# Splitting 220 of 493 weight blocks with GpSimd's transfers: a rounding load, then an accumulating one

## The chip, the cores and the metric

The program runs on one core of one Trainium2 chip. The core has TensorE (PE, matrix multiplications), VectorE (DVE), ScalarE (ACT), GpSimd (POOL) and SyncE (SP, which in this program only issues transfers), and 16 DMA engines that all transfers share, whichever engine issues them. Each engine works off its own queue in order and waits for the others by semaphores. The metric is the device time of one execution in microseconds (us); lower is better.

## What is computed

One sequence of 512 tokens and width 1024 goes through two blocks. The first has two layers, each a feed-forward (SwiGLU) half step, a mixer and another feed-forward half step, each behind a modulated RMS norm; the mixer of layer 0 is stick-breaking attention, that of layer 1 a gated linear recurrence. The second block has two hybrid layers, each one large projection, three kinds of attention, gates, and an output projection.

```python
def first_block(...):
    for layer in range(2):
        mod = (silu(c) @ mod_w[layer] + mod_b[layer]).reshape(B, 3, 3, 1024)
        h, g = sublayer_input(x, norm_g[layer, 0], mod[:, 0])
        x = x + 0.5 * g * swiglu(h, ffn_w_gu[layer, 0], ffn_w_down[layer, 0])
        h, g = sublayer_input(x, norm_g[layer, 1], mod[:, 1])
        y = stick_breaking_attention(h, sb_w_qkv, sb_w_o) if layer == 0 else rglru_block(h, lru_w_in, ..., lru_w_out)
        x = x + g * y
        ...                       # and a second swiglu like the first
def hybrid_layer(x, norm_g, w_in, w_br_a, w_br_b, w_br_c, w_out, cos, sin):
    proj = rmsnorm_2(x, norm_g) @ w_in
    ...                           # ya, yb, yc: block-sparse, top-k and dilated attention, each times a silu gate
    merged = gates_a * (ya @ w_br_a) + gates_b * (yb @ w_br_b) + gates_c * (yc @ w_br_c)
    return x + merged @ w_out
```

## The kernel before

The work is transposed: channels stand on the 128 partitions, the 512 tokens along the row. Every matrix product is made nearly exact in three passes. A float32 operand is split into a high part, rounded to the matmul format F32R, and a low part, the rest; `proj` then issues high·high, high·low and low·high into one PSUM bank.

The weights come as a stream. `layout` puts all weights, in the order of use, into blocks of 128 x 1024 float32 (512 KB, eight slots of 128 x 128 each); between them stand 144 blocks of the modulation's matrix, which DVE reduces (L485). The eight stages in order are ffn00, sb (attention), ffn01, ffn10, lru (recurrence), ffn11, hy0, hy1 (hybrid layers).

- `stream_dma` loads the next blocks: SP issues a transfer into a tile `raw`, of which there are four (`RAW = 4`), as soon as one is free (L463).
- `stream_step` splits the next half block (128 x 512): ACT rounds it into `wh` (L497), then POOL or DVE subtracts, `wl` = `raw` - `wh` (L503). Which of the two it is goes by `pool_low`: 1.0 in sb, in most of lru and in the hybrid layers (all to POOL), 0 in the bodies of the feed-forward stages (all to DVE). `wh` and `wl` have five buffers each (`AHEAD + 1`). When both halves are split, the `raw` is free for the next load.
- `take` hands a slot's `wh` and `wl` to a matmul, and before that has the half blocks up to four ahead of it split (`AHEAD = 4`).

So half block c+4 goes into the buffers that half block c-1 leaves, and TensorE starts on it four half blocks after it has left them. The rest of the work (attention units, gates, norms) runs as generators whose instructions are put among the matmuls; a scheduler at build time, which goes by its own estimates of durations, then fixes each engine's order. In sb an attention unit computes two sigmoids on ACT, masks a diagonal block on POOL (`affine_select`, L1132), scans and multiplies on DVE (L1133, L1137) and goes back to TensorE (transposes `T`, products `o`). In the hybrid layers a pair's projection is rotated on DVE (`sw`, `r`, `rL`: L1362 to L1375, with `rH` on ACT), stacked by SP's transfers (`qs`, `ks`, `kl`, L981) and scored into `z` on TensorE, which DVE masks and reduces (L1399). At the end of a hybrid layer come some 29 blocks that are nothing but projections, with sums on POOL (`sig`, L1816).

Of the kernel before, what the change touches and what calls it, by code (L numbers as in the profile page):

```python
# [22 lines left out]
F32 = mybir.dt.float32  # L23
F32R = mybir.dt.float32r
I32 = mybir.dt.int32
AF = mybir.ActivationFunctionType
OP = mybir.AluOpType
# [149 lines left out]
def first_slots(segs):  # L177

    out = {}
    slot = 0  # L180
    for name, jobs, _ in segs:
        for job in jobs:
            for kt in rows_of(job):
                for j, (_, _, cols) in enumerate(job[1]):
                    if name in LATE and job[0] == "first":
                        out[slot] = (LATE[name], kt, j)
                    elif name == "ffn00" and job[0] in ("gu6", "gu7"):
                        out[slot] = ((0, 0), kt, int(job[0][2:]))
                    slot += len(cols) // 128
    return out  # L190


def rows_of(job):
    return range(job[2]) if isinstance(job[2], int) else job[2]
# [120 lines left out]
class Kern:  # L315
# [117 lines left out]
    def stream_init(self, entries):  # L433
        self.entries = entries
        self.e_dma = 0
        self.e_conv = 0
        self.raws = {}
        self.parts = {}
        self.slot = 0
        self.w_conv = 0  # L440
        self.n_w, self.kept = 0, []
        self.in_ring = 0
        self.full = set()
        self.wshift = {}
        self.inv = None
        self.look = self.AHEAD
        self.act_busy = False
        self.pool_low = 0.0
        self.pool_credit = 0.0

    def stream_dma(self):
        nc = self.nc
        while self.e_dma < len(self.entries):
            src = self.io["ws"][self.e_dma]
            e = self.entries[self.e_dma]
            if e[0] == "w" and self.n_w < self.KEEP:
                raw = [self.t("keep"), self.t("keep")]
                self.n_w += 1
                for j in range(2):
                    nc.sync.dma_start(raw[j], src[:, 512 * j:512 * j + 512])  # L460
            elif self.in_ring < self.RAW:
                raw = self.wpool.tile([128, 1024], F32, name=self.name("raw"), tag="raw", bufs=self.RAW)
                nc.sync.dma_start(raw, src)  # L463
                self.in_ring += 1
                if e[:2] == ("mod", (0, 0, 1)):
                    x = self.t("x")
                    nc.sync.dma_start(x, self.io["xT"][e[2]])
                    if e[2] == 4:
                        nc.sync.dma_start(self.ident, self.io["k_ident"])
                    self.x.append(x)  # L470
            else:
                break
            self.raws[self.e_dma] = raw
            self.e_dma += 1

    def stream_step(self):
        self.stream_dma()
        e = self.entries[self.e_conv]
        raw = self.raws[self.e_conv]
        nc = self.nc  # L480
        if e[0] == "mod":
            vec, m = e[1], e[2]
            if vec not in self.mods:
                self.mods[vec] = self.modp.tile([128, 8], F32, name=self.name("mod"), tag="mod", bufs=12)
            nc.vector.tensor_tensor_reduce(raw, raw, self.cact, 1.0, 0.0, OP.mult, OP.add, accum_out=self.mods[vec][:, m:m + 1])  # L485
            self.full.add((vec, m))
            if m == KD - 1 and vec != (0, 0, 1):
                self.mod_end(vec, 0, KD)
        else:
            j = self.w_conv % 2  # L490
            w = raw[j] if type(raw) is list else raw[:, 512 * j:512 * j + 512]
            h = self.wpool.tile([128, 512], F32R, name=self.name("wh"), tag="wh", bufs=self.AHEAD + 1)
            l = self.wpool.tile([128, 512], F32R, name=self.name("wl"), tag="wl", bufs=self.AHEAD + 1)
            if self.act_busy:
                nc.vector.tensor_copy(h, w)
            else:
                nc.scalar.copy(h, w)  # L497
            self.pool_credit += self.pool_low
            eng = nc.vector
            if self.pool_credit >= 1.0:  # L500
                self.pool_credit -= 1.0
                eng = nc.gpsimd
            eng.tensor_tensor(l, w, h.bitcast(F32), OP.subtract)  # L503
            self.parts[self.w_conv] = (h, l)
            if type(raw) is list:
                self.kept.append((4 * self.w_conv, w))
            else:
                self.shifts(w, 4 * self.w_conv)
            self.w_conv += 1
            if j == 0:  # L510
                return
        if type(raw) is not list:
            self.in_ring -= 1
        del self.raws[self.e_conv]
        self.e_conv += 1
        self.stream_dma()
# [41 lines left out]
    def take(self, n):  # L558
        c, o = divmod(self.slot, 4)
        self.ahead(c)  # L560
        self.parts.pop(c - 1, None)
        self.slot += n
        h, l = self.parts[c]
        return h[:, 128 * o:128 * (o + n)], l[:, 128 * o:128 * (o + n)]
# [1334 lines left out]
    def body(self):  # L1899
        nc = self.nc  # L1900
        segs = segments()
        self.stream_init(layout(segs))
        self.segs = {n: list(j) for n, j, _ in segs}
        self.late = first_slots(segs)
        self.mods = {}
        self.twice = False
        self.quick = False
        self.sq = {}
        self.gain, self.save, self.hnext, self.xd = None, False, [], []
        self.vecs = self.const.tile([128, NVEC], F32, name="vecs")  # L1910
        self.ident = self.const.tile([128, 128], F32, name="ident")
        self.ones = self.const.tile([128, 128], F32, name="ones")
        self.cact = self.const.tile([128, 1024], F32, name="cact")

        def shown(name):
            if self.upto == name:
                for m in range(KD):
                    nc.sync.dma_start(self.io["out"][m], self.x[m])
                return True

        for l in range(2):
            for i in range(2):
                self.jobs = self.segs[f"ffn{l}{i}"]
                if (l, i) == (1, 1):
                    self.twice = self.save = True
                    self.fgain = self.modp.tile([128, 8], F32, name="gain")
                    nc.vector.tensor_tensor(self.fgain, self.vec("final_norm_g"), self.vec("norm_g_2", 0, 8), OP.mult)
                self.ffn(l, i)
                if shown(f"ffn{l}{i}"):
                    return  # L1930
                if i:
                    continue
                if l == 0:
                    self.jobs = self.segs["sb"]
                    self.stick()
                else:
                    with self.tc.manual_schedule():
                        self.lru_consts()
                    self.jobs = self.segs["lru"]
                    self.lru()  # L1940
                if shown("sb" if l == 0 else "lru"):
                    return
        self.hybrid_consts()
        for l in range(2):
            self.jobs = self.segs[f"hy{l}"]
            self.hybrid(l)
            if shown(f"hy{l}"):
                return
        self.last_norm()
# [28 lines left out]
```

## Time and profile before

| | us |
|---|---|
| median of 3 runs | 3132.27 (3131.87 to 3133.31) |
| the profiled execution | 3133.14 |
| its span, first to last instruction | 3131.3 |
| TensorE busy in it | 3007.2 |
| VectorE busy | 1921.7 |
| ScalarE busy | 1321.7 |
| GpSimd busy | 1072.8 |

A profile gives for each engine when each instruction ran; an instruction's idle time before it is put down to what released it. Matmuls overlap each other, so their mean duration (0.39 us) is longer than their distance.

### The profile page before, as it was taken

What the parts mean: (1) busy time and instruction counts of PE and PEld (TensorE: products, weight loads), DVE (VectorE), ACT (ScalarE), POOL (GpSimd) and SP (SyncE); (2) the same over time, 40 slices, a digit from 0 to 9 for tenths busy, and PEclk for the clock granted to TensorE, in tenths of its full rate; (3) what the DMA queues carried; (4) which work ended last, traced back from release to release, by engine and by line L of the source; (5) the groups of instructions that cost most, each with busy time, mean ns of one, the idle gap of its engine ahead of it and who ended that gap; (6) DMA issues with size and microseconds to landing.
All of it is one profiled execution on the core that took longest, in us unless ns stands there. A gap on an engine that the chain in (4) does not pass through costs nothing. (4 is left out here: it accounts for less than half of the span.)

```text
span 3131.3 us, 39192 instructions
## 1 busy us (share of the span) xinstructions
PE 3007.2 (96%) x13752; PEld 2474.4 (79%) x13752; DVE 1921.7 (61%) x3455; ACT 1321.7 (42%) x2520; POOL 1072.8 (34%) x828
## 2 busy tenths in 40 slices
PE   7999999989999999999899999999999999999998
PEld 5788877778888888887788888888787778878776
DVE  7844467685445654569773334587766547877643
ACT  3332245543332333226543333355455434655552
POOL 4455744440001100025430002433334674333356
PEclk9999999999999999999999999999999999999999
DMA  6454545324343344542222223543441336324322
GB/s 243 163 195 172 209 120 142 102 68 147 130 140 128 135 162 149 181 175 74 88 88 101 94 105 111 136 135 105 120 132 62 108 124 177 103 88 128 102 78 91
DMA packets 132358, 400.03 MB, mean 128 GB/s; under 512 B 18496, under 2 KB 19008, under 8 KB 132160
## 3 DMA queue, kind: packets, MB, share of 16 engines
q1 hardware_dynamic: 132160, 397.51, 39.1%
q8 instruction: 109, 1.79, 0.2%
q14 instruction: 89, 0.73, 0.1%
HBM read 342.91 MB, written 6.30 MB: 112 GB/s over the span
## 5 line engine op out<-in xcount | busy, mean ns | idle before, releaser
L503 POOL TENSOR_TENSOR wl<-raw,wh 128x512 fp32r<-128x512 f32 x576 | 803.0, 1402 | 940.9 <-ACT wh L497 897.2
L497 ACT CAST wh<-raw 128x512 fp32r<-128x512 f32 x968 | 596.4, 620 | 1152.7 <-PE mm L417 993.0
L417 PE MATMUL mm<-hH,wh 128*128 128x512 f32 x1584 | 620.9, 392 | 12.4 <-ACT ge L1284 9.8
L417 PE MATMUL mm<-hL,wh 128*128 128x512 f32 x1584 | 620.3, 392 | 4.1 <-DVE hL L722 3.4
L417 PE MATMUL mm<-hH,wl 128*128 128x512 f32 x1584 | 619.4, 391 | 0.3 <-POOL wl L503 0.3
L503 DVE TENSOR_TENSOR wl<-raw,wh 128x512 fp32r<-128x512 f32 x394 | 290.0, 737 | 363.0 <-ACT wh L497 360.6
L417 PE MATMUL mm<-gH,wh 128*128 128x512 f32 x1016 | 409.7, 403 | 1.9 <-ACT wh L497 1.8
L417 PE MATMUL mm<-gH,wl 128*128 128x512 f32 x1016 | 401.9, 396 | 1.3 <-POOL wl L503 1.3
L417 PE MATMUL mm<-gL,wh 128*128 128x512 f32 x1016 | 401.6, 395 | 0.0
L417 PEld LDWEIGHTS mm<-hH,wh 128*128 128x128 f32 x1584 | 299.1, 189 | 76.0 <-ACT ge L1284 10.2
L417 PEld LDWEIGHTS mm<-hL,wh 128*128 128x128 f32 x1584 | 299.0, 189 | 68.5 <-DVE hL L722 5.5
L417 PEld LDWEIGHTS mm<-hH,wl 128*128 128x128 f32 x1584 | 298.9, 189 | 62.3 <-POOL wl L503 0.7
L485 DVE CUSTOM_DVE_ANT_0 raw<-raw,cact 128x1024 f32<-128x1024 f32 x144 | 209.2, 1456 | 177.4 <-DMA raw<-ws 167.0
L417 PE MATMUL mm<-aH,wh 128*128 128x512 f32 x704 | 273.9, 389 | 0.0
L417 PE MATMUL mm<-aH,wl 128*128 128x512 f32 x704 | 273.9, 389 | 0.0
L635 POOL TENSOR_TENSOR sq<-x 128x512 f32<-128x512 f32 x7 | 8.1, 1151 | 736.9 <-DVE x L970 710.0
L417 PEld LDWEIGHTS mm<-gH,wl 128*128 128x128 f32 x1016 | 192.4, 189 | 42.1 <-POOL wl L503 2.6
L417 PEld LDWEIGHTS mm<-gH,wh 128*128 128x128 f32 x1016 | 193.4, 190 | 36.2 <-ACT wh L497 2.3
L417 PEld LDWEIGHTS mm<-gL,wh 128*128 128x128 f32 x1016 | 193.3, 190 | 32.9
L1029 DVE TENSOR_TENSOR wide<-T,wide 128x128 fp32r<-128x128 f32 (+3 forms) x192 | 94.2, 511 | 102.5 <-ACT wide L1026 93.8
L417 PEld LDWEIGHTS mm<-aH,wh 128*128 128x128 f32 x704 | 132.1, 188 | 27.6
L417 PEld LDWEIGHTS mm<-aH,wl 128*128 128x128 f32 x704 | 132.1, 188 | 27.4
(302 smaller groups left out, 4825.0 us busy)
## 6 DMA issues: line engine op xcount, KB each, us to landing
raw<-ws SPq DMA_DIRECT2D x629, 512.0 KB, 3.3
ks<-rH SPq DMA_DIRECT2D x80, 128.0 KB, 3.1
kl<-rL SPq DMA_DIRECT2D x80, 128.0 KB, 2.4
qs<-rH SPq DMA_DIRECT2D x56, 128.0 KB, 3.9
qs<-rL SPq DMA_DIRECT2D x56, 128.0 KB, 3.9
keep<-ws SPq DMA_DIRECT2D x16, 256.0 KB, 5.7
ks<-qkH SPq DMA_DIRECT2D x32, 128.0 KB, 2.8
kl<-qkL SPq DMA_DIRECT2D x32, 128.0 KB, 2.4
```

The lines of the kernel that those rows point to most:

```text
L417: self.nc.tensor.matmul(out, lhsT, rhs, start=start, stop=stop, skip_group_check=True)
L485: nc.vector.tensor_tensor_reduce(raw, raw, self.cact, 1.0, 0.0, OP.mult, OP.add, accum_out=self.mods[vec][:, m:m + 1])
L497: nc.scalar.copy(h, w)
L503: eng.tensor_tensor(l, w, h.bitcast(F32), OP.subtract)
L635: nc.gpsimd.tensor_tensor(q, self.x[m], self.x[m], OP.mult)
L1029: nc.vector.tensor_tensor(dst(pt[1], o, n, step), src(c, n, step), dst(pt[0], o, n, step).bitcast(F32), OP.subtract)
```

## The change

In the four stages sb, lru, hy0 and hy1, 220 blocks are handled in another way: all but those in which a slot also goes into the shift vectors of a norm (`late`). Their load is issued by POOL, with F32R as its destination, so that the transfer itself rounds: the tile `raw` is then the high part, and no `wh` is written. For each half, ACT writes minus the high part into `wl` (`scalar.mul` by -1.0), and a second transfer, issued by POOL too, reads the same half block from HBM again and adds it into `wl`. The `raw` tile now holds what the matmuls read, so it goes back to the ring not when it is split but when `take` has gone past its second half (`held`).

Counted over the program, 422 subtractions on POOL and 18 on DVE go, and 440 roundings on ACT become 440 multiplications (2 of the roundings stood on DVE). SP issues 220 loads less. POOL issues 660 transfers, 220 of 512 KB and 440 of 256 KB, where it issued none. 110 MiB more are read from HBM.

```diff
+def inlined(segs, entries, names, late):
+    out = set()
+    ...
+    for i, e in enumerate(entries):
+        if e[0] != "w":
+            continue
+        name = next((name for end, name in ends if slot < end), None)
+        if name in names and not any(slot + j in late for j in range(8)):
+            out.add(i)
+        slot += 8
+    return out
...
+            elif e[0] == "w" and self.in_ring < self.RAW and self.inline(self.e_dma):
+                raw = self.wpool.tile([128, 1024], F32, name=self.name("raw"), tag="raw", bufs=self.RAW)
+                nc.gpsimd.dma_start(raw.bitcast(F32R), src)
+                raw = (raw, src)
+                self.in_ring += 1
...
+    INLINE = "sb", "lru", "hy0", "hy1"
+    def inline(self, e):
+        return e in self.inlined
...
+            if type(raw) is tuple:
+                h = raw[0].bitcast(F32R)[:, 512 * j:512 * j + 512]
+                l = self.wpool.tile([128, 512], F32R, name=self.name("wl"), tag="wl", bufs=self.AHEAD + 1)
+                nc.scalar.mul(l, h.bitcast(F32), -1.0)
+                nc.gpsimd.dma_start(l, raw[1][:, 512 * j:512 * j + 512], accum_op=OP.add)
+                self.parts[self.w_conv] = (h, l)
+                self.w_conv += 1
+                if j == 0:
+                    return
+                self.held.append(self.w_conv)
+                del self.raws[self.e_conv]
+                self.e_conv += 1
+                self.stream_dma()
+                return
...
         self.parts.pop(c - 1, None)
+        while self.held and self.held[0] <= c:
+            self.held.pop(0)
+            self.in_ring -= 1
+        self.stream_dma()
```

POOL's queue near the end of hy0's attention, where the projections begin (`sig` are the sums of the gated branches). Before:

```order
L1816 TENSOR_TENSOR sig_17890<-sig_17890,sig_19706 128x512
L503 TENSOR_TENSOR wl_20310<-raw_20030,wh_20309 128x512
L1816 TENSOR_TENSOR sig_17995<-sig_17995,sig_19790 128x512
L503 TENSOR_TENSOR wl_20340<-raw_20030,wh_20339 128x512
L1816 TENSOR_TENSOR sig_18245<-sig_18245,sig_19876 128x512
L1816 TENSOR_TENSOR sig_18348<-sig_18348,sig_19954 128x512
L503 TENSOR_TENSOR wl_20375<-raw_20093,wh_20374 128x512
```

The same place of the changed kernel (its lines have other numbers: L483 is the rounding load, L527 the accumulating one, L1866 the sum):

```order
L1866 TENSOR_TENSOR sig_17713<-sig_17713,sig_19479 128x512
L483 DMA raw_20068<-ws 128x1024
L527 DMA wl_20065<-ws 128x512
L1866 TENSOR_TENSOR sig_17813<-sig_17813,sig_19561 128x512
L1866 TENSOR_TENSOR sig_18058<-sig_18058,sig_19645 128x512
L527 DMA wl_20096<-ws 128x512
L1866 TENSOR_TENSOR sig_18156<-sig_18156,sig_19721 128x512
L483 DMA raw_20131<-ws 128x1024
L1866 TENSOR_TENSOR sig_18383<-sig_18383,sig_19788 128x512
L527 DMA wl_20128<-ws 128x512
```

Where two subtractions stood for a block, three issues stand, a load first; the load waits for TensorE to leave the block four before it, the accumulating one for ACT's multiplication, and the sums wait behind them.

POOL's queue in sb, between the masks of the attention units. Before:

```order
L503 TENSOR_TENSOR wl_5386<-raw_5073,wh_5385 128x512
L1132 AFFINE_SELECT beta_5353<-beta_5353 128x128
L1132 AFFINE_SELECT beta_5402<-beta_5402 128x128 x2
L503 TENSOR_TENSOR wl_5428<-raw_5073,wh_5427 128x512
L503 TENSOR_TENSOR wl_5481<-raw_5140,wh_5480 128x512
```

And in the changed kernel (L1182 is the mask):

```order
L527 DMA wl_5465<-ws 128x512
L1182 AFFINE_SELECT beta_5482<-beta_5482 128x128
L483 DMA raw_5497<-ws 128x1024
L527 DMA wl_5494<-ws 128x512
L1182 AFFINE_SELECT beta_5482<-beta_5482 128x128
L1182 AFFINE_SELECT beta_5529<-beta_5529 128x128
```

A mask can now stand behind a load that waits for TensorE.

## Rows read from the trace of the kernel before

**Rows 1.** The page, part 1: each engine's busy time, share of the span, instructions.
```profile
PE 3007.2 (96%) x13752; PEld 2474.4 (79%) x13752; DVE 1921.7 (61%) x3455; ACT 1321.7 (42%) x2520; POOL 1072.8 (34%) x828
```

**Rows 2.** Windows (sb, lru, ffn11, hy0, hy1): PE, PEld, DVE, ACT, POOL busy, clock, DMA share, GB/s.
```profile
403.00:671.00 268.00, 250.61 (x1210) 204.77 (x1209) 190.07 (x309) 144.07 (x286) 119.48 (x128) 0.97 0.40 111
...
1405.00:1610.00 205.00, 187.78 (x807) 152.66 (x806) 162.41 (x193) 111.54 (x176) 98.25 (x68) 0.96 0.24 84
1610.00:1973.00 363.00, 362.73 (x1612) 300.43 (x1611) 155.98 (x225) 124.33 (x204) 39.88 (x29) 1.00 0.29 102
1973.00:2537.00 564.00, 540.44 (x2601) 444.34 (x2600) 383.05 (x884) 284.42 (x620) 254.85 (x195) 0.99 0.39 114
2537.00:3114.00 577.00, 560.04 (x2683) 461.01 (x2681) 369.17 (x857) 283.11 (x618) 272.18 (x213) 0.99 0.36 110
```

**Rows 3.** TensorE's waits in lru: us in total, times, longest.
```profile
PE mm L417 <- ACT ge L1284: 9.8, 1, 9.8
PE z L417 <- DVE xL L1252: 4.2, 1, 4.2
...
PE T L417 <- POOL wl L503: 0.7, 1, 0.7
```

**Rows 4.** TensorE's waits in hy0.
```profile
PE z L417 <- DVE mx L1399: 5.0, 5, 2.3
PE T L421 <- ACT T L1417: 3.5, 8, 0.9
PE o L417 <- DVE diag L663: 2.7, 1, 2.7
...
PE z L417 <- DMA ks<-rH: 0.5, 1, 0.5
```

**Rows 5.** POOL's groups in hy0: count, busy us, mean ns, idle before.
```profile
L503 POOL TENSOR_TENSOR wl<-raw,wh 128x512 fp32r<-128x512 f32 x159 | 214.8, 1355 | 306.2 <-ACT wh L497 294.7 <-PE mm L417 3.5 <-PE o L417 3.2
```

**Rows 6.** DVE's groups in hy0, two that read two SBUF tiles, one PSUM.
```profile
L1366 DVE TENSOR_TENSOR sw<-sw,rope 128x512 f32<-128x512 f32 x24 | 27.5, 1146 | 0.0
L1375 DVE TENSOR_TENSOR rL<-r,rH 128x512 fp32r<-128x512 f32 x24 | 26.6, 1110 | 10.8 <-ACT rH L1373 10.6
...
L1029 DVE TENSOR_TENSOR wide<-T,wide 128x512 fp32r<-128x512 f32 x24 | 16.5, 686 | 27.6 <-ACT wide L1026 27.6
```

**Rows 7.** DVE in ffn10, two SBUF tiles read, while POOL has little to do.
```profile
L928 DVE TENSOR_TENSOR aL<-a,aH 128x512 fp32r<-128x512 f32 x10 | 6.9, 692 | 0.8
```

**Rows 8.** Timeline in hy0: start us, us, engine, line, instruction.
```profile
2042.89 2.98 POOL L503 TENSOR_TENSOR wl<-raw,wh 128x512 fp32r<-128x512 f32 x2 [2.73 <-ACT wh L497]
...
2043.19 1.53 DVE L1366 TENSOR_TENSOR sw<-sw,rope 128x512 f32<-128x512 f32 x1
...
2044.65 1.77 DVE L1375 TENSOR_TENSOR rL<-r,rH 128x512 fp32r<-128x512 f32 x1
```

**Rows 9.** Timeline of ACT in hy0's projections.
```profile
2477.07 0.62 ACT L497 CAST wh<-raw 128x512 fp32r<-128x512 f32 x1 [2.11 <-PE mm L417]
...
2479.78 0.62 ACT L497 CAST wh<-raw 128x512 fp32r<-128x512 f32 x1 [1.11 <-PE mm L417]
2482.51 0.62 ACT L497 CAST wh<-raw 128x512 fp32r<-128x512 f32 x1 [2.11 <-PE mm L417]
```

**Rows 10.** Timeline of POOL at the same place.
```profile
2480.48 1.29 POOL L503 TENSOR_TENSOR wl<-raw,wh 128x512 fp32r<-128x512 f32 x1 [1.42 <-ACT wh L497]
```

**Rows 11.** DMA issues of the whole span: count, KB each, median us to landing.
```profile
raw<-ws SPq DMA_DIRECT2D x629, 512.0 KB, 3.3
...
kl<-rL SPq DMA_DIRECT2D x80, 128.0 KB, 2.4
```

**Rows 12.** The tile raw, late in hy0: duration ns of SP's issue, min/median/max.
```profile
L463 SPq DMA_DIRECT2D raw<-ws x18: 327/328/390, 2410.1 to 2526.0; - x18
```

**Rows 13.** Window with the densest small transfers, the start of hy0.
```profile
1973.00:2100.00 127.00, 121.70 (x628) 103.77 (x627) 88.29 (x215) 58.90 (x124) 53.03 (x42) 1.00 0.58 148
```

**Rows 14.** ACT's groups in lru: loads of a function table, count, busy us, mean ns.
```profile
L1277 ACT ACT_TABLE_LOAD x4 | 5.1, 1283 | 0.1
```

More of the change, by code (lines that the diff above doesn't have):

```diff
@@ L189, in first_slots @@
                     slot += len(cols) // 128
+    return out
+def inlined(segs, entries, names, late):
+    out = set()
+    ends = []
+    n = 0
+    for name, jobs, _ in segs:
+        n += sum(len(cols) // 128 for job in jobs for _ in rows_of(job) for _, _, cols in job[1])
+        ends.append((n, name))
+    slot = 0
+    for i, e in enumerate(entries):
[5 more added lines that the diff above has]
+        slot += 8
     return out
@@ L446, in stream_init @@
         self.look = self.AHEAD
+        self.held = []
         self.act_busy = False
@@ L1904, in body @@
         self.late = first_slots(segs)
+        self.inlined = inlined(segs, self.entries, self.INLINE, self.late)
         self.mods = {}
```

## The prediction

> **What bounds the kernel now.** I read the page first: TensorE is busy 96% of the span [rows 1], so only what shortens TensorE's waits can gain, and whatever adds waits costs. Then the windows by stage: the feed-forward stages leave it next to nothing (362.73 of 363 us in ffn11), and the change leaves them alone. In the four stages that it touches, the waits are 268 - 250.6 = 17.4 us in sb, 17.2 in lru, 23.6 in hy0 and 17.0 in hy1, 75.2 together [rows 2]. That is all there is to gain. Third, the waits: hardly any is for a weight. In lru the long ones are for the recurrence's own chain, and one of 0.7 us for `wl`; in hy0 they are for DVE's masks and reductions, ACT's softmax, a norm's factors [rows 3, 4]. Weights are ready early: in pure projections ACT rounds a half block every 2.72 us, as soon as TensorE has left the buffer, and POOL's subtraction ends 2.0 us later (2479.78 to 2480.48 + 1.29), while TensorE wants it after four half blocks, 4 x 2.72 = 10.9 us [rows 9, 10]. So the split as such is hidden, and the change must gain or lose through its side effects.
>
> **Part by part: what goes.** POOL's subtractions took 1.36 us each in hy0, 215 us of its 255 [rows 2, 5]. POOL waits for TensorE's releases most of the time, so its own time is worth nothing. But DVE pays: with two SBUF tiles to read, its 512-wide operation takes 0.69 us where POOL is nearly idle [rows 7], 1.15 and 1.11 us in hy0, where an operation that reads PSUM still takes 0.69 [rows 6]. The timeline shows how: two subtractions run on POOL from 2042.89 to 2045.87, and `sw` and `rL` on DVE take 1.53 and 1.77 us beside them [rows 8]. These two groups alone lose 24 x (1.15 + 1.11 - 2 x 0.69) = 21 us in hy0.
>
> How much of that reaches TensorE? The operations that TensorE waits for are mostly not stretched themselves, they stand behind one that is. A wait for the masked scores is 5.0 / 5 = 1.0 us [rows 4], a stretch 1.11 - 0.69 = 0.42 us on the mean [rows 6, 7]; if six in ten waits stand behind a stretched operation, a quarter goes. A quarter of 75.2 is **-19 us**; bounds 0 (DVE's time is off the path) and -40 (half the waits go).
>
> **What is replaced at no price.** ACT's rounding, 0.62 us [rows 9], becomes a multiplication of the same 512 columns; nothing. SP's issues fall away; SP bounds nothing, TensorE's waits for its stacks are 0.5 us in hy0 [rows 4]. Two more loads of a function table stand in ACT's order in lru, 1.28 us each [rows 14], **+3 us** at most; I take all of it.
>
> **What is added: the chain behind a half block.** No transfer issued by POOL and none that accumulates is in this trace, so both get bounds. Issue: between 0.33 us, what SP takes [rows 12], and 1.29 us, what POOL took for its subtraction [rows 10]; I take 0.8, and two of them one behind the other, since the load can stand before the accumulating one. Landing: 2.4 us for 128 KB, 3.3 for 512 KB issued by SP [rows 11]. An accumulating 256 KB reads source and destination, so I price it as 512 KB: 3.3 us. Sum: 0.62 + 1.6 + 3.3 = 5.5 us against 10.9, hidden. Upper bound: both issues at 1.29 and the landing behind that of a load, 0.62 + 2.6 + 6.6 = 9.8, still hidden, with 1.1 us to spare: there the cover is thin. The load itself is issued when TensorE leaves a block and wanted three blocks, 6 x 2.72 = 16.3 us, later, after 0.8 + 3.3 for itself and 5.5 for what follows. **0 us**, and the risk goes into a rival.
>
> **The transfer engines.** In ffn11, nearly all loads of blocks, 102 GB/s take a share of 0.29, so a full engine set moves 352 GB/s; in the densest mix of small transfers 148 at 0.58, 255 GB/s [rows 2, 13]. A block of 0.52 MB takes 1.5 us of the set now. Its two accumulations take between 1.5 us (like a plain load) and 4.1 us (twice the bytes at 255 GB/s); taken 3.0, twice at 352. So 4.5 us (3.0 to 6.2) stand against 5.44 us a block in pure projections, and 564 / 82 = 6.9 on hy0's mean, where 0.39 x 6.9 - 1.5 = 1.2 us a block of other transfers come on top. Taken: 83% full in both, enough. At the upper bound it isn't.
>
> The Trainium skill, "Collectives: The Full Stack", section "The bandwidth ceiling: the fold count and why AG ≠ RS ≠ AR", says that an add in the transfer engines costs no cycles of its own but two source reads on one ring, so half the rate. By that an accumulation counts twice, which is what I took from the rows; had it counted once, the block would cost 3.0 us. No row before shows one.
>
> **Sum.** -19 + 3 = -16 on the profiled execution's 3133.1: 3117; the median of the runs shown is 0.9 lower, so **3116 us**, with its own range of 3100 to 3126.
>
> **The rivals.**
> 1. *The low part comes late* (slower). Place: the pure projections of hy0, hy1 and lru, and wherever stacks fill the transfer queues. It decides from 10.9 us from TensorE's release to landing, or 5.44 us of transfer engines a block. For it: my upper bounds are 9.8 and 6.2 us, and all prices are borrowed from SP's transfers; every issue also waits in one in-order queue with POOL's sums and masks. Against it: the middle values are 5.5 and 4.5. Price: at 6.2 us a block, 0.75 us on some 110 blocks of pure projections is +83, so 3132 - 16 + 83 = 3199; with rounding at half rate too it is 3.0 + 4.1 = 7.1 us, 8.3 with the 1.2 of other transfers, and 164 hybrid blocks at 1.4 us over the mean give +230.
> 2. *The gain doesn't arrive.* DVE's freed 21 us a hybrid layer lie in queue time that TensorE never sees, or issuing on POOL stretches DVE as subtracting did. For it: the longest wait of all, 9.8 us, ends with ACT [rows 3]. 3132 to 3135.
> 3. *POOL's queue gets in the way.* A load waits at its head for TensorE, and sb's masks and the hybrid sums stand behind it. For it: before, the subtractions waited too, but with 306 us of idle time in hy0 [rows 5] no one was behind them for long. If a third of the 75 us of waits grow by as much again, +25 - 16: 3141.
> 4. *More gain.* Half the waits go, -40 + 3: 3095.
>
> The Trainium skill, "SBUF — State Buffer", section "SBUF: two separate sides", has a rule against the change: while DVE runs an operation in its two-port mode, such as an fp32 copy in SBUF, GpSimd can't write the descriptors of its transfers, and they start late. Here that would add to rival 1's chain, one DVE operation of up to 0.69 us for each of two issues [rows 7]: 9.8 + 1.4 = 11.2 us at the upper bound, past 10.9; 6.9 at the middle, hidden. No row here shows it, since nothing was issued there.
>
> **How the numbers follow.** Forecast 0.37, rival 4 0.10, rival 2 0.15, rival 1 0.30, rival 3 0.08. Faster or slower by 0.2% is 6 us, about what a measurement of this kernel can tell. Faster: 0.37 + 0.10 = 0.47; same: 0.15; slower: 0.30 + 0.08 = 0.38. The range runs from 3085, under rival 4, to 3205, just over rival 1's first price; it leaves out its heavier form and what is better than rival 4.
>
> **What would show it.** Right: no `wl` subtraction on POOL in the four stages but those near their starts; `sw` and `rL` near 0.69 us; an accumulating transfer landing within 4 us of its issue; TensorE's waits in hy0 and hy1 at 30 us together instead of 41, none worth naming on `wl` or `raw`. Wrong: waits of TensorE on transfers into `wl`, ACT's multiplication waiting for `raw`, a share of the transfer engines near 0.9 in the projections (rival 1); unstretched DVE and unchanged waits (2); masks or sums on POOL idle behind an issue (3).

## The result, and the profile after

The changed kernel takes **3165.24 us** (median of 4 runs, 3153.11 to 3167.03) against 3132.79 for the kernel before beside it: ratio 1.0091, 95% interval 1.0075 to 1.0106. Slower by 32 us, where 16 us faster was forecast. The profiled execution took 3167.03, its span is 3165.2.

Part 1 of its page (as [rows 1]):

```profile
PE 3018.0 (95%) x13752; PEld 2479.5 (78%) x13752; DVE 1804.7 (57%) x3435; ACT 1324.1 (42%) x2524; POOL 994.7 (31%) x1066
```

The windows of sb, lru, ffn11, hy0 and hy1, columns as in [rows 2]:

```profile
406.00:681.00 275.00, 255.37 (x1212) 208.03 (x1211) 175.96 (x311) 145.04 (x286) 105.87 (x157) 0.95 0.72 161
1413.00:1616.00 203.00, 187.54 (x804) 151.51 (x803) 124.13 (x174) 115.50 (x179) 95.39 (x109) 0.97 0.74 153
1616.00:1982.00 366.00, 364.48 (x1613) 301.81 (x1612) 155.94 (x224) 124.47 (x204) 45.07 (x35) 1.00 0.32 103
1982.00:2558.00 576.00, 543.31 (x2601) 445.46 (x2600) 354.71 (x884) 283.58 (x619) 220.58 (x273) 0.99 0.84 183
2558.00:3148.00 590.00, 561.26 (x2682) 462.71 (x2681) 338.12 (x857) 283.05 (x619) 239.93 (x295) 0.99 0.86 184
```

Two things happened at once. VectorE is relieved (hy0: 383 to 355 us busy, hy1: 369 to 338). But TensorE waits more: length less busy time is 19.6 + 15.5 + 32.7 + 28.7 = 96.5 us in the four stages, against 75.2 in [rows 2], and the transfer engines stand at 0.72 to 0.86. The stages grow by 7 us (sb), 12 and 13 us (the hybrids); lru is 2 shorter.

Half of TensorE's waits now end with a transfer: 48.8 of the 96.5 us in the four stages, against 1.6 us before. Two thirds of them are for weights (`wl` and `raw`, 33.5 us) and a third for stacks (15.3 us, 9.9 of them in sb). The waits on transfers (us, times, longest):

```profile
PE mm L436 <- DMA wl<-ws: 27.6, 19, 4.7
PE z L436 <- DMA kl<-qkL: 6.3, 3, 2.9
PE mm L436 <- DMA raw<-ws: 3.6, 1, 3.6
PE z L436 <- DMA ks<-qkH: 3.6, 2, 3.1
PE z L436 <- DMA kl<-rL: 3.0, 2, 1.5
PE z L436 <- DMA qs<-rL: 2.4, 1, 2.4
PE T L436 <- DMA wl<-ws: 1.2, 1, 1.2
PE o L436 <- DMA wl<-ws: 1.1, 1, 1.1
```

The DMA issues of the page (count, KB each, median us to landing) show how long a transfer now takes: `kl` lands in 7.0 us for 2.4 in [rows 11], `ks` in 6.3 for 3.1, `qs` in 5.1 for 3.9.

```profile
raw<-ws POOLq DMA_DIRECT2D x220, 512.0 KB, 5.3
wl<-ws POOLq DMA_DIRECT2D x440, 256.0 KB, 5.4
ks<-rH SPq DMA_DIRECT2D x80, 128.0 KB, 6.3
kl<-rL SPq DMA_DIRECT2D x80, 128.0 KB, 7.0
qs<-rH SPq DMA_DIRECT2D x56, 128.0 KB, 5.1
```

The two DVE groups of [rows 6] in hy0 are short again, so the stretching was GpSimd's subtractions:

```profile
L1425 DVE TENSOR_TENSOR rL<-r,rH 128x512 fp32r<-128x512 f32 x24 | 19.5, 813 | 32.7 <-ACT rH L1423 32.7
L1416 DVE TENSOR_TENSOR sw<-sw,rope 128x512 f32<-128x512 f32 x24 | 16.3, 680 | 0.0
```

And longer waits stand on ScalarE (12.6 us for `raw` before), whose multiplication needs the rounding load:

```profile
ACT wl L526 <- DMA raw<-ws: 142.0, 48, 8.9
ACT wh L543 <- DMA raw<-ws: 35.4, 12, 7.1
```

### The profile page after: what moved, and what is told of

It is laid out like the page before. It is cut to its first block, busy times and chain, and to the rows that moved or that the text cites. A ratio compares the mean times of both kernels' runs of the same rounds, so it can differ in the third digit from the quotient of the medians.

```text
span 3165.2 us, 39232 instructions
## 1 busy us (share of the span) xinstructions
PE 3018.0 (95%) x13752; PEld 2479.5 (78%) x13752; DVE 1804.7 (57%) x3435; ACT 1324.1 (42%) x2524; POOL 994.7 (31%) x1066
## 3 DMA queue, kind: packets, MB, share of 16 engines
q0 software_dynamic: 95040, 230.73, 35.3%
## 5 line engine op out<-in xcount | busy, mean ns | idle before, releaser
L543 ACT CAST wh<-raw 128x512 fp32r<-128x512 f32 x530 | 326.1, 620 | 785.7 <-PE mm L436 679.9
L527 POOL DMA_DIRECT2D wl<-ws x440 | 385.7, 911 | 591.7 <-ACT wl L526 566.1
L436 PE MATMUL mm<-hH,wh 128*128 128x512 f32 x1248 | 486.0, 390 | 0.0
L526 ACT ACTIVATE wl<-raw 128x512 fp32r<-128x512 f32 x440 | 273.1, 629 | 444.8 <-PE mm L436 243.2
L436 PE MATMUL mm<-gH,raw 128*128 128x512 f32 x892 | 362.3, 406 | 1.3 <-DVE sig L1860 1.3
L436 PE MATMUL mm<-gL,raw 128*128 128x512 f32 x892 | 354.2, 397 | 0.0
L549 POOL TENSOR_TENSOR wl<-raw,wh 128x512 fp32r<-128x512 f32 x154 | 227.8, 1494 | 198.2 <-ACT wh L543 183.2
L436 PEld LDWEIGHTS mm<-hL,wh 128*128 128x128 f32 x1248 | 234.7, 188 | 53.2 <-DVE hL L772 4.6
L483 POOL DMA_DIRECT2D raw<-ws x220 | 136.0, 618 | 315.1 <-PE mm L436 252.8
L436 PEld LDWEIGHTS mm<-gH,raw 128*128 128x128 f32 x892 | 170.7, 191 | 31.4 <-DVE sig L1860 2.2
L436 PEld LDWEIGHTS mm<-gL,raw 128*128 128x128 f32 x892 | 170.6, 191 | 28.2
```

The lines of the kernel that those rows point to most:

```text
L436: self.nc.tensor.matmul(out, lhsT, rhs, start=start, stop=stop, skip_group_check=True)
L483: nc.gpsimd.dma_start(raw.bitcast(F32R), src)
L526: nc.scalar.mul(l, h.bitcast(F32), -1.0)
L527: nc.gpsimd.dma_start(l, raw[1][:, 512 * j:512 * j + 512], accum_op=OP.add)
```

## The experiments

**Two runs that take the two halves apart.** `e1_no_sub`: the kernel before without the subtractions. (In the code of all runs, `...` stands for lines left out.)

```diff
-            eng.tensor_tensor(l, w, h.bitcast(F32), OP.subtract)
+            if self.e_conv in self.inlined:
+                l = h
+            else:
...
+                eng.tensor_tensor(l, w, h.bitcast(F32), OP.subtract)
```

> The kernel before, with the subtractions of the 220 blocks left out: the matmuls read the high part a second time where they read the low part, so the low part of these weights is missing from the result. No transfer is added. It sizes the relief of DVE alone. Theory (relief is worth what TensorE's other waits lost in the changed kernel, 75 to about 48 us): 3132 - 27 = 3105 us, 3098 to 3115, with TensorE's waits in sb, lru, hy0 and hy1 at 45 to 55 us and `sw` and `rL` near 0.69 us. Rival (DVE's time is off the path, and the waits of the changed kernel only moved to the transfers): 3126 to 3134 us, though `sw` and `rL` are short.

Measured: 3065.55 us, ratio to before 0.9776 (0.9763 to 0.9790). The relief is 70 us, over twice what the theory gave. Over the four stages TensorE's waits for VectorE fall from 44 us to 12 and those for ScalarE from 26 to 13; for GpSimd it had hardly waited (1.6 us). So most of the relief comes by way of VectorE.

`e2_no_acc`: the changed kernel without its accumulating transfers.

```diff
-                nc.gpsimd.dma_start(l, raw[1][:, 512 * j:512 * j + 512], accum_op=OP.add)
```

> The changed kernel without the accumulating transfers: `wl` stays minus the high part, so the low part of these weights is wrong. Rounding loads, their place in GpSimd's queue, the ring of four held tiles and ScalarE's multiplication all stay. Theory (the accumulating transfers fill the transfer engines and make stacks and low parts late): the stacks `ks`, `kl`, `qs` land within 4 us of their issue again, the share of the transfer engines in hy0 and hy1 falls from 0.85 to 0.5 or less, and the time is that of the relief, 3103 to 3115 us. Rival (the loads in GpSimd's in-order queue, held back by the ring, cost it): TensorE's waits on ScalarE's multiplication and on masks stay, 3125 to 3150 us.

Measured: 3068.92 us, ratio 0.9791 (0.9777 to 0.9804). So rounding loads, the ring of held tiles and their place in GpSimd's queue cost next to nothing, the relief is 66 us, and **the accumulating transfers, with all that waits for them, cost 3165 - 3069 = 96 us**. Its windows (sb, lru, hy0, hy1):

```profile
409.00:660.00 251.00, 244.56 (x1209) 200.77 (x1208) 170.50 (x309) 144.51 (x286) 55.40 (x99) 0.99 0.44 116
1393.00:1582.00 189.00, 182.93 (x806) 149.75 (x805) 124.56 (x175) 112.19 (x177) 48.36 (x53) 0.99 0.28 87
1945.00:2486.00 541.00, 533.18 (x2601) 443.80 (x2600) 344.56 (x884) 285.69 (x620) 85.75 (x114) 1.00 0.43 118
2486.00:3050.00 564.00, 553.93 (x2683) 460.18 (x2681) 332.31 (x856) 284.33 (x618) 93.94 (x126) 1.00 0.43 115
```

TensorE's waits here are 6.4 + 6.1 + 7.8 + 10.1 = 30.4 us, 45 less than before, and its busy time is 1514.6 us for 1538.9, another 24 less, for the same matmuls. About half of the second part is the clock: by its records, the granted clock stood at 0.50 for 47.8 us of these stages before (TensorE busy in 40.7) and for 17.0 us here (15.5). At half the clock a busy microsecond does about half the work (12 matmuls for 23 in 5 us, below), so (40.7 - 15.5) / 2 = 12.6 us go with it; what the other half is was not found. In lru of the changed kernel TensorE waits 4.75 us for a `wl`, until 1525.20. Windows before the wait, right behind it, and later show what follows:

```profile
1515.00:1520.40 5.40, 3.78 (x16) 2.53 (x14) 5.02 (x8) 5.36 (x10) 0.58 (x2) 1.00 0.61 146
1525.20:1530.20 5.00, 5.00 (x12) 3.94 (x13) 4.23 (x7) 2.58 (x5) 1.27 (x2) 0.50 1.06 186
1531.00:1536.00 5.00, 5.00 (x23) 4.10 (x22) 2.35 (x4) 3.36 (x6) 1.84 (x3) 1.00 0.61 148
```

Behind the wait the granted clock is 0.50 (1.2 of 2.4 GHz) and 12 matmuls start in 5 us, later 23. That wait cost 4.75 us and some 2.5 more.

Stage by stage the changed kernel is 99 us longer than `e2_no_acc` in the four windows: 32 us are waits on `wl` and `raw`, 13 waits on stacks, 21 other waits, and 33 more busy time for the same matmuls, 22 of them by the clock, worked out as above.

**Runs that were to split the 96 us, and showed ScalarE's queue.** `e3_acc_scratch`:

```diff
-    NSLOT = 74
+    NSLOT = 72
...
             eng.tensor_tensor(l, w, h.bitcast(F32), OP.subtract)
+            if self.e_conv in self.inlined:
+                src = self.io["ws"][self.e_conv][:, 512 * j:512 * j + 512]
+                nc.gpsimd.dma_start(self.scratch[self.w_conv % 2], src, accum_op=OP.add)
```

> The kernel before, complete, plus the 440 accumulating transfers of 256 KB, each issued behind its subtraction into one of two scratch tiles that nothing reads (72 tiles in the arena for 74 to make room). Nobody waits for these transfers. Theory (the transfer engines' queueing is the loss, and the stacks its first victim): the stacks land at 5 to 7 us for 2.4 to 3.1, TensorE waits 10 to 25 us longer on `ks`, `kl` and `qs`, 3143 to 3160 us. Rival (only the low parts' own chain is late; the stacks are hidden): 3132 to 3138 us, what the issues on GpSimd cost.

Measured: 3644.57 us, ratio 1.1625 (1.1609 to 1.1640), outside both. The transfers depended on no weight, only on the scratch tile, so they were not paced with TensorE; GpSimd's waits and TensorE's:

```profile
POOL scratch L525 <- DMA scratch<-ws: 613.2, 374, 5.5
```

```profile
PE mm L436 <- POOL wl L522: 360.8, 18, 311.3
```

The subtractions of hy0 stood in GpSimd's queue behind transfers that waited for each other, and TensorE stood once for 311.3 us. The run says nothing of contention, but how dear a waiting issue in an in-order queue can be.

`e4_look66` (`NSLOT`: tiles of 128 x 512 in the arena that the rest of the work draws on):

```diff
-    NSLOT = 74
+    NSLOT = 70
...
-    RAW = 4
+    RAW = 6
...
+    LOOK = 6
...
+                tag = ("wh", "wl")[j]
...
+        while (self.w_conv < c + 1 + self.LOOK and self.e_conv in self.raws and type(self.raws[self.e_conv]) is tuple
+               and self.look == self.AHEAD and all(i in self.single for i in range(c, self.w_conv))):
             self.stream_step()
```

> The changed kernel with more time for the same transfers: six `raw` tiles for four, and the low parts of inlined blocks started up to six half blocks ahead for four, in the buffers of `wh` and `wl` in turn (70 tiles in the arena for 74). Same transfers, same bytes. Theory A (the chain of the low part is too long for its cover; its queueing varies): TensorE's waits on `wl` and `raw`, 33 us of the 49 on transfers, nearly go, those on stacks stay: 3132 to 3145 us. Theory B (the transfer engines are full, more time doesn't help, or the earlier start makes the stacks later still): 3158 to 3175 us. Theory C (all of the loss was the short cover): 3105 to 3120 us.

Measured: 3394.49 us, ratio 1.0816 (1.0793 to 1.0839), worse than any theory. `e5_unread`:

```diff
-                self.parts[self.w_conv] = (h, l)
+                self.parts[self.w_conv] = (h, h)
```

> The changed kernel with all its transfers, but the matmuls read the high part a second time where they read the low part of the 220 blocks; the low parts are written and never read (they are missing from the result). So no wait of TensorE on `wl` is left, and the load on the transfer engines stays. Without any accumulating transfer the time is 3069 us, with them 3165 us: 96 us to be split. Theory (late low parts are the smaller part; the stacks, the raw blocks that ScalarE waits for, and the clock that falls with the waits are the larger): 3115 to 3145 us, with waits on `ks`, `kl` and `qs` in sb and the hybrids still near 16 us. Rival (the low part's own lateness is nearly all of it): 3069 to 3085 us.

Measured: 3551.20 us, ratio 1.1323 (1.1304 to 1.1341), outside both. `e6_whole`:

```diff
+                h = raw[0].bitcast(F32R)
+                l = self.wpool.tile([128, 1024], F32R, name=self.name("wl"), tag="w", bufs=self.AHEAD + 1)
                 nc.scalar.mul(l, h.bitcast(F32), -1.0)
...
+                nc.gpsimd.dma_start(l, raw[1], accum_op=OP.add)
...
```

> The changed kernel with one accumulating transfer of 512 KB a block in place of two of 256 KB (rows of 4 KB for 2 KB), one multiplication of 1024 columns in place of two of 512, in tiles that take the place of `wh` and `wl` with the same bytes. Theory A (an accumulating row has a fixed price, so a 4 KB row costs less than two of 2 KB at 178 ns): the share of the transfer engines in the hybrids falls to 0.65 to 0.75, and the time to 3100 to 3140 us. Theory B (the price goes by bytes): rows of 350 ns, the share stays at 0.84, 3150 to 3180 us, the longer transfers weighing against the fewer issues.

Measured: 3443.09 us, ratio 1.0985 (1.0963 to 1.1006), outside both. In these three the same row of ScalarE's waits grew; here that of `e4_look66`, of `e5_unread` and of `e6_whole`:

```profile
ACT wl L529 <- DMA raw<-ws: 396.1, 105, 16.7
```

```profile
ACT wl L526 <- DMA raw<-ws: 853.1, 184, 12.5
```

```profile
ACT wl L526 <- DMA raw<-ws: 711.0, 171, 11.8
```

From 52.1 us in `e2_no_acc` (3069) over 142 in the changed kernel (3165) to 396 (3394), 711 (3443) and 853 (3551), a longer wait goes with a longer time, though not in proportion. In the changed kernel the multiplication waits for a buffer that TensorE must leave, which keeps it late. With more buffers, or with buffers that nobody reads, that hold is gone: in `e5_unread` it waits for TensorE 7.2 us in 5 places, in the changed kernel 243.2 us in 174. It then stands earlier in ScalarE's order, which the build fixes by its own estimates. ScalarE comes to it a median of 6.0 us after its load's issue in the changed kernel, but of 2.5, 2.2 and 1.9 us in `e4_look66`, `e6_whole` and `e5_unread`, and the load takes 5.3 to 6.2 us to land. Casts and softmax queue behind it: in `e5_unread` TensorE waits 83.7 us, 34 times, for softmax values `T` from ScalarE. So none of the three tells late low parts from load. `e6_whole` does tell the price: its queue of GpSimd's transfers took 30.3% of 16 engines' 3443.5 us; with the rounding rows as in `e2_no_acc` (13.0% of 3066.8 us for 28,160 of them, 0.23 us each), an accumulating 4 KB row takes (16694 - 6380) / 28160 = 0.37 us, and one of 2 KB in the changed kernel (35.3% of 3165.2 us) (17877 - 6380) / 56320 = 0.20 us. The price goes by bytes, as theory B had it.

`e7_alternate`:

```diff
-        return e in self.inlined
+        return e in self.inlined and e % 2 == 0
```

> The changed kernel with only every second of the 220 blocks split by transfers, the others by ScalarE and GpSimd as before. Theory (the relief goes by the number of subtractions that leave GpSimd, half of 66 us; the loss by queueing, which falls faster than the load): 3100 to 3125 us, share of the transfer engines in the hybrids about 0.62, stacks landing at 3 to 5 us. Rival (both halve): (3133 + 3165) / 2 = 3149 us. Rival (GpSimd's in-order queue suffers from the mixture: subtractions behind loads that wait for TensorE): over 3150 us.

Measured: 3156.54 us, ratio 1.0070 (1.0055 to 1.0085), over the theory, 8 us over the rival in which both halve, and in the range of the last one, whose reason (GpSimd's queue) the run with six tiles below speaks against. The stacks are better (`kl` 5.2 us, `ks` 4.0), but now the blocks that ScalarE rounds wait for their loads, since a held tile keeps the ring of four full:

```profile
ACT wh L543 <- DMA raw<-ws: 234.7, 69, 11.7
```

`e8_dve_half`:

```diff
-                eng = nc.gpsimd
+                eng = nc.vector if self.w_conv // 2 % 2 else nc.gpsimd
```

> The kernel before without any new transfer: where GpSimd subtracted, every second block's two subtractions go to VectorE instead. Theory (GpSimd's subtractions cost VectorE more in stretched operations than VectorE would need to do them itself): each one moved adds 0.69 us to VectorE and takes away a stretch of up to 1.1 us that hits some of its operations; 3105 to 3132 us. Rival (VectorE's own queue is what TensorE waits behind, and 75 us more work in each hybrid layer lengthens it): 3135 to 3170 us.

Measured: 3130.39 us, ratio 0.9991 (0.9982 to 1.0000). It lies at the upper edge of the theory's range: VectorE pays about what it gets.

**More lead for the loads.** `e9_raw5`, whose edit is shown, `e10_raw6` (6 and 70 in place of 5 and 72) and the same six with every second block, `e11_alt_raw6`:

```diff
-    NSLOT = 74
+    NSLOT = 72
...
-    RAW = 4
+    RAW = 5
```

> The changed kernel with five `raw` tiles for four (72 tiles in the arena for 74): each load is issued one block, about 5.4 us, earlier against ScalarE's multiplication, and nothing else changes; the same transfers and bytes. Theory (ScalarE's in-order queue is where the time goes: its multiplication waits for the rounding load, and softmax, casts and gates wait behind it): ScalarE's waits on `raw` fall from 177 us to under 60, TensorE's waits on transfers and on ScalarE fall with them, 3105 to 3140 us. Rival (the transfer engines are too full, whatever the order: loads issued earlier queue longer and make stacks later): 3155 to 3185 us.

> As the run with five tiles, with six (70 tiles in the arena): loads two blocks, about 10.9 us, earlier than in the changed kernel. Theory (ScalarE's queue): ScalarE's waits on `raw` nearly gone, 3095 to 3130 us; what is left above 3069 us is the stacks' and the low parts' own lateness. Rival (full transfer engines): 3155 to 3190 us. A third way (70 tiles are too few, TensorE waits for attention units that wait for tiles): over 3150 us with short waits of ScalarE on `raw`.

> Every second block split by transfers, as in the alternating run (3157 us, where ScalarE waited 235 us for `raw`, since a held tile keeps the next load back), with six `raw` tiles and 70 in the arena. Theory (ScalarE's queue): its waits on `raw` fall below 40 us and the time to 3085 to 3115 us, under both kernels: half the relief of 66 us, and stacks that land at 3 to 5 us. Rival (queueing or the mixture on GpSimd decides): 3135 to 3160 us.

Measured: 3148.18 us (ratio 1.0048, 1.0035 to 1.0060), 3149.29 us (1.0053, 1.0041 to 1.0066) and **3122.57 us (0.9972, 0.9962 to 0.9982)**. The first one's waits of ScalarE on `raw` all but vanish:

```profile
ACT wh L543 <- DMA raw<-ws: 16.2, 5, 6.7
ACT wl L526 <- DMA raw<-ws: 9.1, 3, 3.4
```

ScalarE now comes to the multiplication 13.4 us after its load's issue. The theory holds in kind, not in size: of the 96 us, 17 go with ScalarE's waits, and a sixth tile gives nothing more. All three times lie between the ranges of theory and rival. With every second block the same lead is worth 34 us: ScalarE's waits on `raw` for `wh` fall from 234.7 us to 36.9, while GpSimd's subtractions wait for TensorE as before (316 and 322 us). That version is faster than both kernels, by less than expected.

**Late low parts or load.** `e12_ahead5`, six `raw` tiles and six half blocks' buffers:

```diff
-    NSLOT = 74
+    NSLOT = 68
...
-    RAW = 4
-    AHEAD = 4
+    RAW = 6
+    AHEAD = 5
```

> The run with six `raw` tiles (3149 us), and six buffers of `wh` and `wl` for five: every half block is split five half blocks ahead for four, so the low part has about 2.7 us more (68 tiles in the arena). ScalarE's multiplication still waits for TensorE's release of a buffer. Theory A (late low parts are the larger part of what is left, 25 us of waits and the clock behind them): TensorE's waits on `wl` under 8 us, 3110 to 3135 us. Theory B (what is left is the queueing of stacks and all else that the transfers make late): waits on `wl` fall, the time by no more than those waits, 3130 to 3150 us. Against both: ScalarE's waits on `raw` grow, since the loads keep less lead: over 3155 us.

Measured: 3150.23 us, ratio 1.0057 (1.0040 to 1.0074). Against `e10_raw6`, the like run with five buffers, the waits on `wl` fall from 25.0 us to 11.6; the time doesn't. By stage, though, lru takes 190.5 us for 204.4 in `e9_raw5`; ffn00, where nothing is split, takes 8 us longer, and each hybrid stage 4. What the recurrence gains, the others lose. `e13_paced`, with five `raw` tiles and `NSLOT = 69`:

```diff
-                nc.gpsimd.dma_start(l, raw[1][:, 512 * j:512 * j + 512], accum_op=OP.add)
+                nc.gpsimd.dma_start(self.scratch[self.w_conv % 3], l.bitcast(F32), accum_op=OP.add)
```

> The changed kernel with five `raw` tiles (3148 us), with the accumulating transfer turned away from the low part: it reads the finished multiplication's 256 KB from SBUF and adds them into one of three scratch tiles that nothing reads (69 tiles in the arena). TensorE reads minus the high part, so the low part of these blocks is wrong. The load on the transfer engines and GpSimd's queue stay, TensorE no longer waits for a landing into `wl`. Theory A (the lateness of low parts decides): 3070 to 3100 us. Theory B (the load itself, which makes stacks and ScalarE's and VectorE's chains late, decides): 3110 to 3145 us, stacks landing at 5 to 7 us.

Measured: 3129.81 us, ratio 0.9989 (0.9978 to 0.9999): theory B. With no landing into `wl` to wait for, the time is 18 us better than `e9_raw5`, 14 of them in lru (204.4 to 190.0 us); the other 61 above `e2_no_acc` stay. They are the price of the load, with two differences that the run brings along: the accumulating transfer reads SBUF in place of HBM, and GpSimd waits 38.4 us for a scratch tile to be free. Its windows of sb, lru, hy0 and hy1, and TensorE's longest waits on transfers:

```profile
404.00:672.00 268.00, 249.14 (x1210) 203.07 (x1209) 170.88 (x309) 144.62 (x286) 104.34 (x153) 0.97 0.72 163
1404.60:1594.60 190.00, 183.80 (x805) 150.64 (x805) 124.83 (x175) 112.23 (x178) 95.29 (x108) 0.98 0.74 163
1957.00:2528.00 571.00, 543.07 (x2605) 447.62 (x2604) 354.30 (x885) 287.07 (x621) 221.83 (x275) 0.98 0.83 185
2528.00:3106.00 578.00, 556.56 (x2680) 460.45 (x2678) 332.69 (x857) 284.29 (x618) 236.24 (x292) 0.99 0.85 187
```

```profile
PE z L436 <- DMA qs<-rL: 12.3, 3, 9.7
PE z L436 <- DMA kl<-qkL: 8.7, 4, 3.4
PE z L436 <- DMA kl<-rL: 5.1, 4, 1.5
PE z L436 <- DMA ks<-qkH: 2.7, 2, 2.6
```

Stage by stage against `e2_no_acc`, the load alone costs 17 us in sb, 30 in hy0 and 14 in hy1, but 1 in lru, at a share of 0.74 against 0.72 in sb. What lru lacks is stacks; that this makes the difference fits, but no run shows it by itself.

`e14_alt_vector` (`e11_alt_raw6`, with the second halves that GpSimd would subtract going to VectorE) and `e15_before_raw6` (the kernel before with six `raw` tiles):

```diff
-                eng = nc.gpsimd
+                eng = nc.vector if j else nc.gpsimd
```

> Every second block split by transfers, six `raw` tiles (3123 us), and of the subtractions that GpSimd still makes the second of each block goes to VectorE, so that GpSimd keeps about a quarter of them. Complete. Theory (what is left of the gain of 66 us goes by the subtractions that leave GpSimd, less VectorE's own 0.69 us each): 3100 to 3120 us. Rival (VectorE's queue pays as much as it gets, as when half of them went to VectorE alone, 3130 us): 3120 to 3130 us.

> The kernel before with six `raw` tiles for four and 70 tiles in the arena: the control for the versions with six. Theory (before, weights come early anyway): 3128 to 3138 us, so that what the alternating version gains comes from the transfers that split. Rival (the ring or the arena by themselves gain or lose): outside of that.

Measured: 3126.39 us (0.9969, 0.9957 to 0.9981), the rival's figure: no better than `e11_alt_raw6`; and 3133.52 us (0.9998, 0.9989 to 1.0007). The ring by itself is worth nothing, so `e11_alt_raw6` owes its gain to the splitting.

`e16_lru_only` and `e17_mix`, on top of `e12_ahead5`:

```diff
-    INLINE = "sb", "lru", "hy0", "hy1"
+    INLINE = "lru",
```

```diff
-        if name in names and not any(slot + j in late for j in range(8)):
+        if name in names and (name == "lru" or i % 2 == 0) and not any(slot + j in late for j in range(8)):
```

> The run with six `raw` tiles and five half blocks ahead (3150 us), with only the recurrence's 28 blocks split by transfers; sb and the hybrids as in the kernel before. The recurrence has no stacks, so a load on the transfer engines has nothing there to make late but the weights themselves, and these have the longer cover. Theory (stacks are the first victims of the load): lru takes 188 to 193 us for 205 before, the other stages as before, 3115 to 3123 us. Rival (the load costs lru as it costs the others): 3128 to 3136 us.

> As the run with the recurrence alone, and every second block of sb and the hybrids as well: lru as there, the others as in the alternating run (265, 562 and 580 us against 268, 565 and 577 before). Theory (gains and losses of the stages add): 3112 to 3122 us. Rival (the sixth buffer's arena of 68 tiles or the longer look costs the mixed stages): 3125 to 3140 us.

Measured: 3147.25 us (1.0031, 1.0020 to 1.0042) and 3149.33 us (1.0041, 1.0028 to 1.0053). The first one's windows of ffn00, lru and hy0:

```profile
13.70:415.40 401.70, 376.84 (x1617) 306.57 (x1616) 233.03 (x325) 123.59 (x212) 219.32 (x148) 0.97 0.54 188
...
1414.00:1604.00 190.00, 182.00 (x804) 149.50 (x803) 130.27 (x177) 112.07 (x177) 95.22 (x106) 0.98 0.78 166
1966.50:2545.60 579.10, 548.97 (x2604) 446.34 (x2603) 381.64 (x885) 286.31 (x621) 258.94 (x196) 0.99 0.38 112
```

lru does what the theory said, 190 us for 205. But both times lie outside all that was expected, since the runs are spoiled elsewhere, as the first one shows: ffn00 and hy0, where nothing is split, take 402 and 579 us for 389 and 564. Six half-block buffers, the longer look or 68 tiles cost that by themselves; which, was not tried. So the time of `e12_ahead5` can't be held against late low parts in the hybrids either; `e13_paced`, with its look of four, stands.

## Why the prediction was wrong

**What bounds the kernel.** That TensorE's waits decide was right, but it took a wait at its own length, so that 75.2 us would be "all there is to gain". Behind the one shown TensorE ran 5 us at half clock, and in the four stages 45 us less of waits came with 24 us less of busy time, about half of it by the clock.

**The relief: the term was mis-sized.** The mechanism was right: without GpSimd's subtractions `sw` and `rL` fall from 1.15 and 1.11 us to 0.68 and 0.81, and TensorE's waits with them. "A quarter of 75.2 is -19 us" should have read six tenths, 45, and with the busy time behind them 66 to 70; the bound of -40 was too near as well. Two readings on the way were off and changed little: without subtractions `rL` takes 0.81 us, not 0.69, so that the two groups lose 18 us, not 21; and POOL's waits in [rows 5] end with ACT's rounding (294.7 of 306.2 us), which in turn waits for TensorE.

**The chain behind a half block: "0 us" was wrong in its tail.** Followed through hy0 of the changed kernel half block by half block, from TensorE's release it takes a median of 0.2 us to the multiplication, 0.9 to the issue, 5.5 to the landing; the median of the whole is 7.2 where I had 5.5, and TensorE wants the result 11.2 us or more after the release, as I had it. But the landing goes up to 11.5 us, and the multiplication comes up to 15.0 us late, for `raw` or other work of ScalarE. Over the program 18 of 439 half blocks were finished under 0.4 us before TensorE read them, or held it up, 14 of them behind a multiplication that came 1.6 to 15.0 us late: 29.9 us of waits. Median values hid the distribution; the upper bound of 9.8 left ScalarE's own lateness out.

**The transfer engines: "83% full in both, enough" is the step that failed.** The load was forecast well: 0.84 and 0.86 measured, 3.3 us for the two accumulations of a block (256 rows at 0.20 us over 16 engines), where I had 3.0. What was wrong is "enough", which put the load at nothing: `e13_paced` has it at 61 us. At that share a stack, wanted as soon as it lands, comes at 5 to 7 us for 2.4 to 3.9, a rounding load at 5.3 us and a low part at 5.4. I had looked at whether the blocks get through, and "SP bounds nothing" dismissed its stacks. Rival 1 had the sign right and named "wherever stacks fill the transfer queues", but priced only the pure projections at an overfull engine set; those, behind hy0's attention (2450 to 2558 us), in fact hold 4.3 us of waits, and only 0.3 of it is for a transfer. The mean also hides where the engines are full, early in a hybrid layer and around the change from one to the next, where blocks meet stacks (columns as in [rows 2]; the second line is of pure projections):

```profile
2032.00:2082.00 50.00, 43.18 (x185) 34.26 (x185) 26.42 (x66) 21.30 (x46) 16.50 (x23) 0.96 1.02 227
2450.00:2532.00 82.00, 78.04 (x357) 63.49 (x356) 44.59 (x68) 35.27 (x69) 47.20 (x52) 1.00 0.85 184
2532.00:2682.00 150.00, 137.11 (x615) 112.61 (x613) 73.34 (x154) 51.59 (x103) 72.57 (x88) 0.97 1.03 224
```

The last stretch has 9 of the 18 late half blocks and 12.9 us of TensorE's waits. [rows 13] had a share of 0.58 at such a place already; with the 3.0 us for each 6.9 us of hy0's mean it comes to about 1.0, an estimate from the prediction's own terms, but its sum took the mean of the stage. That 3165 lies between 3085 and 3205 is luck: the range reached so far for overfull engines in the pure projections, where the share is 0.85.

**The sum.** By the medians: relief -66; the ring that makes ScalarE wait +17 (`e9_raw5`); late low parts +18 (`e13_paced`, 14 of them in lru); the load +61; together +30, against +32 measured. Each term is the step from one run to the next, so that they add up by construction; they size the terms in this order, and adding up proves nothing. Of the 61, TensorE's waits on stacks in `e13_paced` are 28.8 us; the rest, as I suppose longer chains through VectorE and ScalarE and the clock behind the waits, was not taken apart. Rival 3 (masks and sums on GpSimd) does not show: TensorE waits for GpSimd's old subtractions alone (3.4 us), and ScalarE's waits for the sums fall from 29.2 us to 21.6. The rival in which the gain doesn't arrive is refuted by `e1_no_sub`. The two loads of a function table came (11 in lru for 9), but their +3 us are not visible in lru, which got shorter.

The Trainium skill, "Collectives: The Full Stack", section "The bandwidth ceiling: the fold count and why AG ≠ RS ≠ AR", has it, for a reduction between cores, that an add needs two source reads and so halves the rate. The rows nearly agree: 0.20 us for 2 KB accumulated against 0.23 for 4 KB rounded, 1.8 times the price per byte. The Trainium skill's rule in "SBUF — State Buffer", section "SBUF: two separate sides", that VectorE's two-port mode can hold up GpSimd's descriptors, no row here shows by itself.

## What to carry to other kernels

A mean share of the transfer engines below 1 is not room: before adding bulk transfers, look for the stretches that are far over the mean, and for small transfers that an engine wants as soon as they land, whose latency here rose from 2.4 to 3.9 us to 5 to 7 at a share of 0.84. A TensorE wait taken away was worth half as much again as it was long, in part since the clock behind it comes back. And on an in-order engine an instruction that waits for a transfer must be held late by something that is sure, or its load given a buffer more of lead, as here with five tiles for four (17 us), or with every second block and six: 3123 us, 0.28% under the kernel before.

## What was not expected of the hardware

- GpSimd's 512-wide subtractions cost this kernel 66 to 70 us, mostly through VectorE, though GpSimd is idle two thirds of the time.
- At 0.84 of the transfer engines the 128 KB stacks `ks` and `kl`, issued by SyncE, land in a median of 6.3 and 7.0 us; with the rounding loads alone, at 0.43, in 4.4 and 4.5.
- An accumulating 4 KB row takes 0.37 us, two of 2 KB 0.40: longer rows save next to nothing.
